# The context scan in a tile of its own, the ada modulation moved from the loop to the LayerNorm stage, late gelus in their own buffers

## The chip, the cores and the metric

One core of a Trainium2 chip runs the kernel. The metric is device time in microseconds of one execution, taken as the median of several; the kernel before took 882.67 us (three runs, 881.9 to 884.6). A core has a matrix engine (TensorE, PE in the profile), three engines for element-wise work (VectorE or DVE, ScalarE or ACT, GpSimd or POOL) and a queue that issues the DMAs here (SyncE, SP). Each engine takes its instructions in the order of the program and they wait for each other through semaphores.

## The reference

One layer of a diffusion backbone over 512 latent tokens with 256 context tokens, width 1024. What is computed, cut to its core:

```python
sh1, sc1, gt1, sh2, sc2, gt2 = split(silu(c) @ w_ada + b_ada)      # the ada modulation, 6 x 1024
hl = rmsnorm(x, g_pre_mix) * (1 + sc1) + sh1                       # hc: the same for the context, with c_ctx
glu, xr, gt, (ga, gb) = split(hl @ w_in)
# RG-LRU, both directions d, context first, then the latent tokens from its last state:
r, i = sigmoid(xr_d @ w_r + b_r), sigmoid(xr_d @ w_i + b_i)        # xr after a conv of width 4
a = exp(-8 * r * softplus(-lam)); u = sqrt(1 - a * a) * i * xr
h[t] = a[t] * h[t - 1] + u[t];  rec = h_forward + h_backward
y_a = silu(layernorm(conv31(v * sigmoid(g)))) @ w_proj_conv
y_b = (rec * gelu(gt)) @ w_proj_lru
x = x + gt1 * rmsnorm((sigmoid(ga) * y_a + sigmoid(gb) * y_b) @ w_out, g_post_mix)
h = rmsnorm(x, g_pre_ffn) * (1 + sc2) + sh2
x = x + gt2 * rmsnorm((silu(g) * v) @ w_down, g_post_ffn)          # v, g: 3x3 depthwise conv of h @ w_up
```

## The kernel before, in words

Channels lie on the 128 partitions, tokens along the free dimension; a width of 1024 is 8 blocks. Every matmul of the network is done in three (mm3, lines 133 to 136): each float32 operand is split into a rounded high part and the remainder, and high x high, low x high and high x low are summed in PSUM. Weights are split on the way in: SP loads a raw tile (line 105, a ring of 3), ACT writes whi (line 122) and POOL, for some DVE, writes wlo = raw - whi (line 123, rings of 4). The function queue lists all weights in one fixed order, and W(key, look, ahead) splits up to `look` weights ahead of the one that is wanted and loads `ahead` further. cvt_to and dma_to do it for one index. The order of every engine's instructions is that of the program text.

PSUM has two tags for matmuls: mm2 (two tiles of two banks) and mm1 (two of one bank); cv tiles (two) belong to the convolution and to small things. A tile that is asked for waits until the last reader of the one whose place it takes. The same holds for SBUF pools that are opened where others were closed: the side "right" is a stack, and with reuse_waits="tile" a new tile waits for the old tiles whose addresses it overlaps.

The stages, in time of the profile: start, norms and first blocks (0 to 100 us); the loop over the eight channel blocks b of the recurrence (lines 665 to 742, 76 to 293 us); gelus, ga, gb, yb (lines 744 to 802, to 402 us); LayerNorm stage (lines 814 to 876, to 442 us); ya and its output projection (to 545 us); the ConvFFN (to the end).

An iteration b of the loop does on PE: block xr for b (24 matmuls of 512 columns and 24 of 262 for the context), gate_mm for block b - 1 (direction 0, r), block v, gate_mm (0, i) and (1, r), block g, gate_mm (1, i). Each gate_mm takes an mm2 tile, as xr does, so xr of b + 1 takes the place of gate (1, r), whose last reader is DVE's L612 of that direction. ACT does the gates' tanh in place (L597), the decay a (L604), another tanh (L605) and a square (L607); the square roots of block b - 2 (L623, with a table load before and after). DVE does conv31 in portions (fill, L520), the width-4 convolution (L568 to L575), L612 and L616, the products L629 and the scans of block b - 2: L634 over the context in place in u, L635 over the latent tokens into rec, starting from the context's last column, L636 backwards over both. POOL does wlo, xl (L140), the other L629 and the sum of both directions (L637).

Inside iterations 2 to 5 a share of the ada modulation (the 1024 values of sh2) is done: two tiles `wa` of weights are loaded (L715, tag wa of pool pl, 8 KB), PE multiplies them into the free quarter of the last gate's PSUM tile (ada_pe, L303), and DVE sums into ggb (L731, L733); iteration 6 transposes the sum into adl (ada_cols, L320, L321). The share sc2 is done in the LayerNorm stage instead: tiles in the place of later w_out weights (ada_dma, L806), two groups of four (ada4), into the PSUM tile acc4.

After the loop gt_act applies gelu to the eight gate branches: 0 to 4 in their SBUF copies, 5 to 7 from PSUM into sa (L653). Then gt_post multiplies with rec (L658) and splits the product on ACT (rgh) and DVE or POOL (rgl, L140) for the yb blocks. offload does a few taps of the convolution on ACT and POOL (L544, L546). ga_act writes tanh of ga into sa (L774).

Of the kernel before, what the change touches and what calls it, by code (L numbers as in the profile page):

```python
# [37 lines left out]
def backbone_kernel(es: ExitStack, tc: tile.TileContext, x, ctxt, par, wadq, wada, win, wgate, wpc, wpl, wout,  # L38
# [459 lines left out]
    pl = es_r.enter_context(tc.tile_pool(name="pl", bufs=2, side="right", reuse_waits="tile"))  # L498

# [131 lines left out]
    def scans(b):  # L631
        (a0, _), (a1, _) = lru[b, 0], lru[b, 1]
        u0, u1 = lru[b, 0, 1], lru[b, 1, 1]
        V.tensor_tensor_scan(u0[:, T:TA], a0[:, T:TA], u0[:, T:TA], 0.0, ALU.mult, ALU.add)  # L634
        V.tensor_tensor_scan(rec[:, b, :], a0[:, 0:T], u0[:, 0:T], u0[:, TA - 1:TA], ALU.mult, ALU.add)  # L635
# [15 lines left out]
    def gt_act(b):  # L651
        t = gts[b] if b < 5 else sa[:, b, :]
        S.activation(out=t, in_=gts[b], func=AF.Gelu_apprx_tanh)  # L653
        gts[b] = t
# [10 lines left out]
    for b in range(1, NB + 1):  # L665
# [46 lines left out]
        if 2 <= b <= 5:  # L712
            for k in (2 * b - 4, 2 * b - 3):
                was[k] = pl.tile([128, D], F32, tag="wa", name="wa")
                nc.sync.dma_start(out=was[k], in_=wada[1, :, k, :])  # L715
# [10 lines left out]
        ps = gate_mm(b - 1, 1, 1)  # L726
        if 2 <= b <= 5:
            o = ps[:, TA:1024]
            ada_pe((2 * b - 4, 2 * b - 3), (was[2 * b - 4], was[2 * b - 3]), o, True, True)
            if b == 2:  # L730
                V.tensor_copy(ggb[:, 0:256], o)  # L731
            else:
                V.tensor_add(ggb[:, 0:256], ggb[:, 0:256], o)  # L733
        if b == 6:
            ada_cols(3, ggb[:, 0:256])(ps[:, T:1024])
# [12 lines left out]
    for b in range(5):  # L748
        gt_act(b)
# [29 lines left out]
    gt_act(5)  # L779
    gt_act(6)  # L780
    gt_act(7)
    gt_post(range(NB))
    offload(4)
    yb = pd.tile([128, NB, T], F32, tag="d", name="yb")
    for b in (0, 1):
        ga_act(b)
    for b in range(-1, NB):
# [16 lines left out]
    def ada_dma(k):  # L804
        was[k] = pw1.tile([128, D], F32, tag=f"wo{k // 2 % 2}{'hl'[k % 2]}", name="wa")
        nc.sync.dma_start(out=was[k], in_=wada[2, :, k, :])  # L806

    def ada4(ks):
        ada_pe(ks, [was[k] for k in ks], acc4[:, 0:256], ks[0] == 0, ks[-1] == NB - 1)
        for k in ks:  # L810
            if k < 4:
                ada_dma(k + 4)

    for b in (2, 3):
# [4 lines left out]
    for k in range(4):  # L819
        ada_dma(k)  # L820
# [19 lines left out]
    ada4(range(4))  # L840
# [9 lines left out]
    ga_mm(5, range(6, NB))  # L850
    ga_mm(6, look=1)
# [8 lines left out]
    for b in range(NB):  # L860
# [6 lines left out]
        if b == 3:  # L867
            ga_mm(7)
# [4 lines left out]
    ada4(range(4, NB))  # L873
# [24 lines left out]
    for b in range(NB):  # L898
# [3 lines left out]
        if b in (0, 3):  # L902
            rest()
# [342 lines left out]
```

## Time and profile before

| | us |
|---|---|
| median of three runs | 882.67 |
| profiled execution, its own time | 883.99 |
| its span, first to last instruction | 882.2 |
| PE busy in the span | 854.5 |
| DVE, ACT, POOL busy | 663.0, 430.7, 412.7 |
| mean granted TensorE clock | 0.993 |

The profile is a record of one execution: for each instruction its engine, line, tiles, start and length, the idle time of the engine before it and what ended that. From it come a list of groups of instructions, a list of waits, the chain of work that ended last, timelines of one engine, and sums over stretches. A matmul's length in the record is longer than the spacing of two, since they overlap; read the starts. The granted clock is 1.00 at 2.4 GHz and 0.50 at 1.2 GHz.

### The profile page before, as it was taken

The numbers are of one execution on the slowest core, as the hardware profiler recorded it, in microseconds if no ns is written. First come the engines' busy times: TensorE is split into PE (matmuls) and PEld (weight loads), VectorE is DVE, ScalarE is ACT, GpSimd is POOL, SyncE is SP. The second block draws the span as 40 slices with busy tenths as digits, with TensorE's granted clock in tenths as the row PEclk, the third lists the DMA queues.
The fourth block names the chain that finished last, engine by engine and source line by source line (L and its number), as shares of the span: only waits on it lengthen the run. The fifth ranks groups of instructions, "written<-read, shape, count | busy, mean of one in ns | idle before, by whom it ended". The sixth has DMA issues, their size and how long they took to land.

```text
span 882.2 us, 11379 instructions
## 1 busy us (share of the span) xinstructions
PE 854.5 (97%) x4312; PEld 691.3 (78%) x4312; DVE 663.0 (75%) x932; ACT 430.7 (49%) x614; POOL 412.7 (47%) x227
## 2 busy tenths in 40 slices
PE   7999999999899889999999999999999999999997
PEld 6777877877787668887778889888888888888785
DVE  4355899999997999994465345899998998998204
ACT  5273766866677742223753345634534344345222
POOL 1234545655456574545343212536645556457820
PEclk9999999999999999999999999999999999999999
DMA  9952133222222222224454411223432333333402
GB/s 351 371 216 84 61 120 132 108 99 68 72 84 72 95 96 96 94 86 156 167 167 144 166 48 48 96 85 119 143 119 85 124 112 112 113 113 124 163 0 96
DMA packets 31398, 106.01 MB, mean 120 GB/s; under 512 B 3440, under 2 KB 3568, under 8 KB 31344
## 3 DMA queue, kind: packets, MB, share of 16 engines
q1 hardware_dynamic: 31344, 105.29, 33.9%
q8 instruction: 34, 0.56, 0.3%
q14 instruction: 20, 0.16, 0.1%
HBM read 103.17 MB, written 2.10 MB: 119 GB/s over the span
## 4 chain that ended last, share of the span: by engine, by line
PE 75%; DVE 11%; ACT 8%; issue 3%; POOL 1%; DMA 0%; DVEq 0%; SPq 0%; ACTq 0%
PE up_ps L135 8%; PE up_ps L134 8%; PE up_ps L136 8%; DVE cv L520 3%; DVE rec L635 3%; PE ya_ps L134 2%; PE y_ps L135 2%; PE yb_ps L136 2%; PE yb_ps L135 2%; PE yb_ps L134 2%; PE ya_ps L136 2%; PE ya_ps L135 2%; PE y_ps L134 2%; PE y_ps L136 2%; PE gb_ps L136 2%
## 5 line engine op out<-in xcount | busy, mean ns | idle before, releaser
L123 POOL TENSOR_TENSOR wlo<-raw,whi 128x1024 fp32r<-128x1024 f32 x117 | 290.4, 2495 | 221.6 <-ACT whi L122 221.4
L1040 DVE SCALAR_TENSOR_TENSOR cv<-zall,P,cv 128x512 f32<-128x512 f32 x240 | 161.8, 743 | 0.2
L520 DVE SCALAR_TENSOR_TENSOR cv<-glu,P,cv 128x512 f32<-128x512 f32 x228 | 153.8, 745 | 0.0
L122 ACT ACTIVATE whi<-raw 128x1024 fp32r<-128x1024 f32 x121 | 125.0, 1052 | 21.0 <-issue 8.0
L134 PE MATMUL up_ps<-Ahi,whi 128*128 128x512 f32 (+1 forms) x352 | 131.8, 374 | 0.0
L135 PE MATMUL up_ps<-Alo,whi 128*128 128x512 f32 (+1 forms) x352 | 131.7, 374 | 0.0
L136 PE MATMUL up_ps<-Ahi,wlo 128*128 128x512 f32 (+1 forms) x352 | 131.6, 374 | 0.0
L135 PEld LDWEIGHTS up_ps<-Alo,whi 128*128 128x128 f32 x352 | 66.0, 188 | 13.3
L136 PEld LDWEIGHTS up_ps<-Ahi,wlo 128*128 128x128 f32 x352 | 66.0, 188 | 13.2
L134 PEld LDWEIGHTS up_ps<-Ahi,whi 128*128 128x128 f32 x352 | 66.0, 188 | 13.1
L1026 POOL TENSOR_TENSOR acl<-fo,ach 128x512 fp32r<-128x512 f32 x20 | 26.0, 1300 | 85.5 <-ACT ach L1023 85.5
L1040 DVE SCALAR_TENSOR_TENSOR cv<-zall,P,cc 128x512 f32<-128x512 f32 x40 | 43.1, 1105 | 21.2 <-ACT cc L1014 21.2
L1012 ACT ACTIVATE zall<-up_ps 128x512 f32<-128x512 f32 x40 | 23.7, 592 | 63.5 <-PE up_ps L136 63.5
L597 ACT ACTIVATE gate_ps<-gate_ps,P 128x768 f32<-128x768 f32 x32 | 27.9, 873 | 47.5 <-DVE ggb L733 19.1
L1023 ACT ACTIVATE ach<-fo 128x512 fp32r<-128x512 f32 x20 | 12.7, 633 | 66.8 <-DVE fo L1022 66.8
L140 POOL TENSOR_TENSOR xl<-xc,xh 128x768 fp32r<-128x768 f32 x8 | 14.9, 1858 | 45.9 <-ACT xh L139 45.9
L364 ACT ACTIVATE tg<-gb_ps 128x512 f32<-128x512 f32 x8 | 4.8, 596 | 60.2 <-PE gb_ps L136 60.2
L134 PE MATMUL xr_ps<-Ahi,whi 128*128 128x512 f32 x56 | 23.3, 416 | 5.6 <-DVE e L612 5.6
L136 PE MATMUL gb_ps<-Ahi,wlo 128*128 128x512 f32 x64 | 26.0, 407 | 2.5 <-POOL wlo L123 2.5
L1014 ACT ACTIVATE cc<-up_ps,P 128x512 f32<-128x512 f32 x40 | 27.3, 682 | 1.8 <-DVE cv L1040 1.8
L1040 DVE SCALAR_TENSOR_TENSOR fo<-zall,P,cv 128x512 f32<-128x512 f32 x40 | 27.8, 734 | 0.0
L134 PE MATMUL ga_ps<-Ahi,whi 128*128 128x512 f32 x64 | 26.0, 406 | 1.6 <-ACT sa L653 1.6
(391 smaller groups left out, 2127.0 us busy)
## 6 DMA issues: line engine op xcount, KB each, us to landing
raw<-in_win_dram SPq DMA_DIRECT2D x48, 512.0 KB, 3.3
raw<-in_wup_dram SPq DMA_DIRECT2D x40, 512.0 KB, 3.3
wa<-in_wada_dram SPq DMA_DIRECT2D x24, 512.0 KB, 5.7
raw<-in_wdn_dram SPq DMA_DIRECT2D x22, 512.0 KB, 3.3
wa<-in_wadq_dram SPq DMA_DIRECT2D x16, 512.0 KB, 8.1
raw<-in_wpl_dram SPq DMA_DIRECT2D x8, 512.0 KB, 3.2
raw<-in_wpc_dram SPq DMA_DIRECT2D x8, 512.0 KB, 3.8
raw<-in_wout_dram SPq DMA_DIRECT2D x8, 512.0 KB, 3.3
```

Source lines behind the costliest of these rows:

```text
L122: S.activation(out=flat(hl[0]), in_=flat(t), func=AF.Copy)
L123: eng.tensor_sub(flat(hl[1]), flat(t), flat(hl[0]))
L134: PE.matmul(o, lh, rh, start=first, stop=False)
L135: PE.matmul(o, lh, rl, start=False, stop=False)
L136: PE.matmul(o, ll, rh, start=False, stop=last)
L520: V.scalar_tensor_tensor(out=cv[b] if k else glu[:, b, 0:T], in0=glu[:, b, k:k + T], scalar=col("dw31", 31 * b + k, 1), in1=cv[b], op0=ALU ...
L597: S.activation(out=lru[b, d, q], in_=lru[b, d, q], func=AF.Tanh, scale=0.5, bias=hb[:, i:i + 1])
L635: V.tensor_tensor_scan(rec[:, b, :], a0[:, 0:T], u0[:, 0:T], u0[:, TA - 1:TA], ALU.mult, ALU.add)
L1012: S.activation(out=z[:, 1:1 + GH, 1:1 + GW], in_=ps.rearrange("p (r c) -> p r c", c=GW), func=AF.Copy)
L1014: S.activation(out=c, in_=ps.rearrange("p (r c) -> p r c", c=GW), func=AF.Copy, scale=col("dw9", 9 * (i + FW * (1 - s)) + 4, 1))
L1026: G.tensor_sub(acl[:, i, :], fo[i, 0], ach[:, i, :])
L1040: V.scalar_tensor_tensor(out=o, in0=zz[i, s][:, k // 3:k // 3 + GH, k % 3:k % 3 + GW], scalar=col("dw9", 9 * (i + FW * (1 - s)) + k, 1), i ...
```

## The change

Four things. scans writes the context scan into a tile hc of its own (1 KB, two buffers in pl) and takes the start value from there. The ada work of sh2 leaves the loop, with its loads, additions and transposes; instead the LayerNorm stage loads all 16 weight tiles in four groups (ada_dma, ada4): sc2 in groups 0 and 1, sh2 in groups 2 and 3, the first loads being issued before ga 2, and each of the two sums is copied out of acc4 and transposed in the ya stage, where rest now runs at b = 0, 1 and 2 instead of 0 and 3. The gelus 5 to 7 go to a new pool pge (three buffers of 2 KB) and all eight follow the last scans in the text, ahead of the new pools. And the split of weight gb 1 is put before gt_post, that of yb 0 after it, both ahead of ga_act and offload.

```diff
--- before.py
+++ after.py
@@ -496,6 +496,7 @@
     block(ps1[:, 0:T], W(("xr", 1), 1, 2), Ahi, Alo)
     es_q.close()
     pl = es_r.enter_context(tc.tile_pool(name="pl", bufs=2, side="right", reuse_waits="tile"))
+    pge = es_r.enter_context(tc.tile_pool(name="pge", bufs=3, side="right", reuse_waits="tile"))
 
 
     lacc = [None]
@@ -631,8 +632,9 @@
     def scans(b):
         (a0, _), (a1, _) = lru[b, 0], lru[b, 1]
         u0, u1 = lru[b, 0, 1], lru[b, 1, 1]
-        V.tensor_tensor_scan(u0[:, T:TA], a0[:, T:TA], u0[:, T:TA], 0.0, ALU.mult, ALU.add)
-        V.tensor_tensor_scan(rec[:, b, :], a0[:, 0:T], u0[:, 0:T], u0[:, TA - 1:TA], ALU.mult, ALU.add)
+        hc = pl.tile([128, TC], F32, tag="hc", name="hc")
+        V.tensor_tensor_scan(hc, a0[:, T:TA], u0[:, T:TA], 0.0, ALU.mult, ALU.add)
+        V.tensor_tensor_scan(rec[:, b, :], a0[:, 0:T], u0[:, 0:T], hc[:, TC - 1:TC], ALU.mult, ALU.add)
         V.tensor_tensor_scan(u1[:, TA - 1::-1], a1[:, TA - 1::-1], u1[:, TA - 1::-1], 0.0, ALU.mult, ALU.add)
         (V if b == 7 else G).tensor_add(rec[:, b, :], rec[:, b, :], u1[:, 0:T])
 
@@ -649,7 +651,7 @@
         gts[b] = t
 
     def gt_act(b):
-        t = gts[b] if b < 5 else sa[:, b, :]
+        t = gts[b] if b < 5 else pge.tile([128, T], F32, tag="ge", bufs=3, name="ge")
         S.activation(out=t, in_=gts[b], func=AF.Gelu_apprx_tanh)
         gts[b] = t
 
@@ -709,10 +711,6 @@
         i_dve(b - 1, 0)
         if b + 1 < NB:
             glu_mul(tg, psv, b + 1)
-        if 2 <= b <= 5:
-            for k in (2 * b - 4, 2 * b - 3):
-                was[k] = pl.tile([128, D], F32, tag="wa", name="wa")
-                nc.sync.dma_start(out=was[k], in_=wada[1, :, k, :])
         if b + 2 < NB:
             psg = mm1("g_ps")
             block(psg, W(("g", b + 2)), Ahi, Alo)
@@ -723,16 +721,7 @@
         fill(3)
         r_dve(b - 1, 1)
         fill(3)
-        ps = gate_mm(b - 1, 1, 1)
-        if 2 <= b <= 5:
-            o = ps[:, TA:1024]
-            ada_pe((2 * b - 4, 2 * b - 3), (was[2 * b - 4], was[2 * b - 3]), o, True, True)
-            if b == 2:
-                V.tensor_copy(ggb[:, 0:256], o)
-            else:
-                V.tensor_add(ggb[:, 0:256], ggb[:, 0:256], o)
-        if b == 6:
-            ada_cols(3, ggb[:, 0:256])(ps[:, T:1024])
+        gate_mm(b - 1, 1, 1)
         gate_tanh(b - 1, 1, 1)
         if not last:
             xcs[b] = xc_new
@@ -745,7 +734,7 @@
     gt_block(7)
     scans_mul(7)
     scans(7)
-    for b in range(5):
+    for b in range(NB):
         gt_act(b)
     es_r.close()
 
@@ -776,14 +765,13 @@
     turn[0] = 1
     ga_mm(0)
     ga_mm(1, look=1)
-    gt_act(5)
-    gt_act(6)
-    gt_act(7)
+    cvt_to(index["gb", 1])
     gt_post(range(NB))
-    offload(4)
+    cvt_to(index["yb", 0])
     yb = pd.tile([128, NB, T], F32, tag="d", name="yb")
     for b in (0, 1):
         ga_act(b)
+    offload(4)
     for b in range(-1, NB):
         if b + 1 < NB:
             psg = mm_any("gb_ps")
@@ -801,23 +789,27 @@
         fill(7)
         offload(2)
     gs2 = const.tile([128, 8], F32, name="gs2")
-    def ada_dma(k):
-        was[k] = pw1.tile([128, D], F32, tag=f"wo{k // 2 % 2}{'hl'[k % 2]}", name="wa")
-        nc.sync.dma_start(out=was[k], in_=wada[2, :, k, :])
-
-    def ada4(ks):
-        ada_pe(ks, [was[k] for k in ks], acc4[:, 0:256], ks[0] == 0, ks[-1] == NB - 1)
-        for k in ks:
-            if k < 4:
-                ada_dma(k + 4)
-
+
+    wk = [(2, k) for k in range(NB)] + [(1, k) for k in range(NB)]
+
+    def ada_dma(n):
+        was[n] = pw1.tile([128, D], F32, tag=f"wo{n // 2 % 2}{'hl'[n % 2]}", name="wa")
+        nc.sync.dma_start(out=was[n], in_=wada[wk[n][0], :, wk[n][1], :])
+
+    def ada4(g):
+        ns = range(4 * g, 4 * g + 4)
+        ada_pe([wk[n][1] for n in ns], [was[n] for n in ns], acc4[:, 0:256], g % 2 == 0, g % 2 == 1)
+        if g < 3:
+            for n in ns:
+                ada_dma(n + 4)
+
+    for n in range(4):
+        ada_dma(n)
     for b in (2, 3):
         ga_mm(b, range(NB if b < 3 else 4))
         fill(7)
     ga_act(2)
     fill(1000)
-    for k in range(4):
-        ada_dma(k)
     mean, acc4 = cv_tile("mean"), cv_tile("ada_cp")
     PE.matmul(mean, ones, lacc[0], start=True, stop=True)
     ga_mm(3, range(4, NB))
@@ -837,7 +829,7 @@
     V.tensor_add(sq[:, 1, :], sq[:, 1, :], sq[:, 7, :])
     V.tensor_add(sq[:, 0, :], sq[:, 0, :], sq[:, 1, :])
     cvt_to(index["ga", 6])
-    ada4(range(4))
+    ada4(0)
     big = cv_tile("var")
     for t in range(4):
         PE.matmul(big[:, t:t + 1], sq[:, 0, 128 * t:128 * t + 128], ones[:, 0:1], start=True, stop=True)
@@ -848,6 +840,8 @@
     spread(big, rv, 4)
     rl = big
     ga_mm(5, range(6, NB))
+    ada4(1)
+    rest4 = ada_cols(4, acc4[:, 0:256], acc4)
     ga_mm(6, look=1)
     ga_act(4)
     ga_act(5)
@@ -865,13 +859,14 @@
         if b > 1:
             ln_lo(b - 2)
         if b == 3:
+            ada4(2)
             ga_mm(7)
         if b == 5:
             cvt_to(index["ya", 0])
     ln_lo(6)
     ln_lo(7)
-    ada4(range(4, NB))
-    rest = ada_cols(4, acc4[:, 0:256], acc4)
+    ada4(3)
+    rest = [rest4, ada_cols(3, acc4[:, 0:256], acc4)]
     for b in (6, 7):
         ga_act(b)
 
@@ -899,11 +894,11 @@
         ps = mm_any("ya_ps")
         block(ps, W(("ya", b), 0), slh, sll)
         cvt_to(index["ya", min(b + 2, 7)] if b < 7 else index["wo", 5])
-        if b in (0, 3):
-            rest()
+        if b < 3:
+            rest[b]()
         ya_post(b, ps)
         if b == 1:
-            rest = ada_rows(2, "g_post_mix", ggb)
+            rest += [ada_rows(2, "g_post_mix", ggb)]
             V.scalar_tensor_tensor(out=gs2, in0=adl[:, 32:40], scalar=1.0, in1=col("g_pre_ffn"), op0=ALU.add, op1=ALU.mult)
     es_s.close()
```

## Rows read from the trace of the kernel before

**Rows 1.** The page, part 1: TensorE's busy time, share of the span, instructions.

```profile
PE 854.5 (97%) x4312; PEld 691.3 (78%) x4312; DVE 663.0 (75%) x932; ACT 430.7 (49%) x614; POOL 412.7 (47%) x227
```

**Rows 2.** Waits of PE: who for whom, total us, times, longest us.

```profile
PE xr_ps L134 <- DVE e L612: 5.6, 5, 1.9
```

**Rows 3.** Timeline of PE, loop: start us, length us, what, [idle before <-releaser].

```profile
100.42 0.39 PE L134 MATMUL xr_ps<-Ahi,whi 128*128 128x512 f32 x1
...
124.44 1.07 PE L303 MATMUL gate_ps<-wa,sT 128*32 128x256 f32 x16
...
125.88 0.50 PE L134 MATMUL xr_ps<-Ahi,whi 128*128 128x512 f32 x1 [0.37 <-DVE e L612]
...
153.04 0.50 PE L134 MATMUL xr_ps<-Ahi,whi 128*128 128x512 f32 x1 [1.12 <-DVE e L612]
```

**Rows 4.** Timeline of ACT, iterations 2 and 4 of the loop.

```profile
110.20 0.88 ACT L597 ACTIVATE gate_ps<-gate_ps,P 128x768 f32<-128x768 f32 x1
...
155.33 0.88 ACT L597 ACTIVATE gate_ps<-gate_ps,P 128x768 f32<-128x768 f32 x1 [6.37 <-DVE ggb L733]
...
164.54 0.86 ACT L597 ACTIVATE gate_ps<-gate_ps,P 128x768 f32<-128x768 f32 x1
```

**Rows 5.** Timeline of DVE, iteration 2 of the loop.

```profile
105.89 1.49 DVE L629 TENSOR_TENSOR u<-u,e 128x768 f32<-128x768 f32 x1 [0.76 <-ACT e L623]
...
115.34 3.24 DVE L635 TENSOR_TENSOR_SCAN rec<-a,u 128x512 f32<-128x512 f32 x1
...
118.50 1.73 DVE L636 TENSOR_TENSOR_SCAN u<-a,u 128x768 f32<-128x768 f32 x1
...
124.89 0.94 DVE L612 SCALAR_TENSOR_TENSOR e<-e,gate_ps 128x768 f32<-128x768 f32 x1
```

**Rows 6.** Timeline of POOL, iteration 2 of the loop.

```profile
114.74 2.76 POOL L123 TENSOR_TENSOR wlo<-raw,whi 128x1024 fp32r<-128x1024 f32 x1 [3.20 <-ACT whi L122]
```

**Rows 7.** Timeline of PE after the loop, ga 1 and gb 1.

```profile
302.47 0.50 PE L134 MATMUL ga_ps<-Ahi,whi 128*128 128x512 f32 x1 [1.58 <-ACT sa L653]
...
313.78 0.40 PE L134 MATMUL gb_ps<-Ahi,whi 128*128 128x512 f32 x1
...
314.01 0.40 PE L135 MATMUL gb_ps<-Alo,whi 128*128 128x512 f32 x1
...
316.95 0.79 PE L136 MATMUL gb_ps<-Ahi,wlo 128*128 128x512 f32 x1 [2.55 <-POOL wlo L123]
```

**Rows 8.** Windows: length; PE, PEld, DVE, ACT, POOL busy; granted clock; DMA.

```profile
234.50:238.10 3.60, 3.59 (x9) 2.81 (x10) 2.58 (x5) 1.56 (x3) 0.00 (x0) 0.53 0.01 2
...
299.40:302.90 3.50, 1.92 (x9) 1.25 (x8) 3.47 (x3) 1.08 (x3) 0.71 (x1) 1.00 0.47 149
...
316.60:320.00 3.40, 3.04 (x7) 2.47 (x8) 3.40 (x5) 0.00 (x0) 3.40 (x3) 0.51 0.44 152
```

**Rows 9.** Timeline of ACT after the loop.

```profile
301.82 1.58 ACT L653 ACTIVATE sa<-gt_ps 128x512 f32<-128x512 f32 x3 [4.19 <-DVE u L636]
...
312.35 2.00 ACT L122 ACTIVATE whi<-raw 128x1024 fp32r<-128x1024 f32 x2
```

**Rows 10.** Timeline of DVE after the loop.

```profile
297.76 3.97 DVE L636 TENSOR_TENSOR_SCAN u<-a,u 128x768 f32<-128x768 f32 x1
...
312.91 4.54 DVE L140 TENSOR_TENSOR rgl<-sa,rgh 128x512 fp32r<-128x512 f32 x2
```

**Rows 11.** The chain that ended last, LayerNorm stage: start, us, what.

```profile
422.53 1.86 PE ada_cp L303 x32
...
426.88 0.89 PE var L329 x8
```

**Rows 12.** DMAs of line 806, second group of weights: issue to landing.

```profile
DMA to landing us min/median/max: 3.5/4.7/5.9
```

**Rows 13.** Timeline of ACT, LayerNorm stage.

```profile
431.12 0.82 ACT L863 ACTIVATE glu<-glu,P 128x512 f32<-128x512 f32 x1
```

**Rows 14.** All DMAs into tiles wa: issue to landing.

```profile
DMA to landing us min/median/max: 2.6/5.3/12.0
```


## Prediction

> **What bounds the kernel now.** I read the page first: TensorE (PE) is busy 97% of a span of 882.2 us [rows 1], so time can come only from where PE waits, from slow PE clock, or from PE work that goes. The list of waits names what PE waited for; the reader is to see there that the largest item is the first xr matmul of a loop iteration waiting for DVE's L612, 5.6 us in 5 waits [rows 2]. Then I laid PE, ACT, DVE and POOL of the loop side by side. Call X(b) the moment PE starts block xr of iteration b: X(2) = 100.42, X(3) = 125.88, X(4) = 153.04 [rows 3], and three more periods like the last (X(5) to X(7)). So iteration 2 took 25.46 us and iterations 3 to 6 took 27.16 us each.
>
> Iteration 2 shows the chain that closes an iteration: xr and the first gate on PE, ACT's L597 at 110.20 = X+9.78 [rows 4], three more ACT steps, DVE's first L612, scans L634 to L636, fillers, second L612 ending at 124.89 + 0.94 = 125.83, and xr of iteration 3 starts 0.05 later [rows 3, 5]. PE itself had finished its own work at 124.44 and then did 1.07 us of the ada modulation [rows 3], which lay inside its wait. In iteration 4 the same L597 stands at 164.54 = X+11.50, 1.72 later, and that is the 1.70 by which the period is longer. The reason is one step back: the last gate's L597 sat idle 6.37 us for DVE's ggb addition (L733), which reads the same PSUM bank, and came only at 155.33 = X+2.29 [rows 4]. From there ACT was the late one.
>
> After the loop PE stands twice more: 1.58 us before ga_mm(1) for a gelu (L653) and 2.55 us for POOL's wlo of gb 1 [rows 7]. The gelu into sa had itself waited 4.19 us for the last scan L636 [rows 9], because sa lies where the loop's tiles lay. The clock counts too: after the wait before X(7) it was granted 0.53 in 234.5 to 238.1, after the wait for wlo 0.51 in 316.6 to 320.0; the wait of 1.58 us left it at 1.00 [rows 8].
>
> **Part 1, ggb out of the loop.** The additions go, so L597 of the last gate starts when PE is done, some 1.3 us ahead of X (PE ready at 124.44, X(3) at 125.88) instead of 2.29 behind it. That is 3.6 us earlier where 1.7 are needed, so ACT is no longer late; next is the chain of iteration 2, 25.46. The 1.07 us of PE work itself brings nothing here: PE then only waits longer, 1.5 us per iteration. What could be late next is DVE with POOL: L629 took 1.49 in iteration 2 beside a wlo of POOL, and POOL's own L629, the other direction's, followed [rows 5]. With ACT earlier, that POOL instruction (as long as a wlo, 2.4 to 2.8 [rows 6]) comes ahead of DVE's; DVE then waits up to about 2 us there instead of 0.55. It has some room (0.76 of it was waiting for the square root), so the period rises by 0 to 0.4. I take 25.65, the middle: 4 x (27.16 - 25.65) = 6.0 us gained, bounds 5.2 and 6.8. The loop's 8 DMAs on SP go too; PE, ACT and DVE show no wait for them.
>
> **Part 2, the clock at X(7).** 3.6 us at 0.53 cost 3.6 x 0.47 = 1.6 us of dense PE work [rows 8]. The wait there was 1.9 [rows 2]; with the change it is 25.65 less PE's own 24.0 (100.42 to 124.44) = 1.65, next to the 1.58 that kept the clock. I take all 1.6, bounds 0 and 1.6. PE sets the pace from there to the end of the loop (the chain of waits is PE's own from 234.5 on), so the gain is passed on.
>
> **Part 3, hc.** The scan L635 took 3.24 us for 512 columns, while L636 did 768 in 1.73 [rows 5]: by that rate it needs 1.2, so 2.0 us are a wait. I read it as POOL's: wlo runs 114.74 to 117.50 [rows 6], and 117.50 + 1.08 is the scan's end. In the last block L636 itself took 3.97 [rows 10] with a wlo beside it. L634 writing its own tile leaves the scan's two SBUF inputs, its wait for L634's result and the order on ACT and POOL as they are. The bounds are 0 and 2.0 us per iteration; I take 0, because the start of that wlo hangs on the same ACT step as the scan. The Trainium skill says the same ("SBUF — State Buffer", "Who interferes with whom"): a DVE instruction with two SBUF inputs contends with a GpSimd instruction that reads SBUF, and the lock is exclusive. It speaks against this part of the change, and the trace agrees: 3.24 beside a POOL instruction, while the 768-column scan without one took 1.73. By the rule this part brings 0; were it wrong, the sum would be that of the first rival.
>
> **Part 4, gelus and weights.** The gelus of gt 5 to 7 follow the first five at once, without L636; ga_mm(1) no longer waits: 1.58. wlo of gb 1 came late because its ACT half ran at 312.35, behind all of gt_post [rows 9]; now it is split ahead, and POOL has it by about 305: 2.55. With these the slow clock of 316.6 to 320.0 goes, 3.4 x 0.49 = 1.6. In sum 5.7. Some is given back. pl loses 8 KB and gains 2, pge takes 6, so the end of that stack is where it was and sa overlaps the new ge buffers: ga_act(0) must wait until gt_post's last subtraction has read them. DVE finished that at 312.91 + 4.54 = 317.45 [rows 10]; the two early wlo's share the port with gt_post (they delay it by about 2.4) and the wlo's and offload additions that delayed it before come later (about as much), so I leave it at 317.5. ACT stands behind it with ga_act, four offload steps and the split of gb 2. PE reaches yb 0 at 302.47 - 1.6 + 3 blocks of 24 matmuls at 0.23 us (5.6 each) = 317.7 [rows 7], needs ga_act(0)'s PSUM tile at 318.3, and then wlo of gb 2, about 1.5 us late by the same count (four offload steps of the size of a gelu, 0.5 or a little more, the split of 1.0 [rows 9], POOL's 2.4 to 2.8). I put both at 1.9 us, bounds 0 (tiles not held) and 3.2. Net 5.7 - 1.9 = 3.8, bounds 2.5 and 5.7.
>
> **Part 5, ada in the LayerNorm stage.** Two more groups of 32 narrow matmuls at 1.86 us [rows 11] on a PE that has no gap there: 3.7, and two transposes and a copy, 0.2; the loop's copy of this work was inside waits, so nothing is set against it. Now the DMAs. Group 2 of weights is issued as group 1's tiles are used, by 422.53 + 1.86 = 424.4, and lands 3.5 to 5.9 us after [rows 11, 12]; the last of four is there by about 430.5. PE reaches ada4(1) at 427.8 + 6 matmuls = 429.2 and its last quarter at 430.6 [rows 11]: no wait to speak of. Groups 3 and 4 have a whole block (5.6) plus 1.4 as cover: 7.0 against 5.9. SP is held by these DMAs, and behind them queue the loads of ya 0 and 1, which ACT wants in the middle of its silus; they may cost ACT 1 to 1.5. The copy R ahead of the LayerNorm loop holds DVE until 431.1 instead of 427.8, but ACT's first silu came only at 431.12 [rows 13], so the chain moves by 1.1 while PE has 3.7 more to do before ya. I take 4.0 lost, bounds 3.9 and 6 (one late landing).
>
> **Sum.** -6.0 - 1.6 - 0 - 3.8 + 4.0 = -7.4. The profiled execution took 883.99 (span 882.2 and 1.8 around it), so 876.6; it stands 1.3 above the median of 882.67, so the forecast for the median is 875.3. After the LayerNorm stage PE is dense to the end, so nothing is lost on the way. The bounds of the terms together give -1.7 to -10.2 if all fall to one side.
>
> **The rivals.**
> (1) hc does free the scan. For: L635 alone among the scans reads a start value that was just written in the same tile. Against: L636's 3.97. Iterations would fall to PE's own 24.0, five of them by 1.6 more: -8, 867.
> (2) DVE becomes the bound in the loop, because POOL meets its two-input steps more often. For: DVE is without a gap in the iterations. Period 26.8 instead of 25.65 leaves 1.4, and the longer PE wait keeps the clock loss: -1.4 - 3.8 + 4.0 = -1.2, 881.5.
> (3) PE's longer waits at each X(b) let the clock fall each time. For: 1.9 did it once. Against: 1.58 did not. Four falls more of 1.6 on the chain and none saved: -6.0 - 3.8 + 4.0 + 6.4 = +0.6, 883.3.
> (4) Slower: ada4(1) to ada4(3) wait for their weights. The place is PE's in-order queue, with ga 6, ga 7 and ya 0 behind. It decides once a landing takes longer than its cover, about 6, 7 and 7 us; the slowest landing of such a tile in the trace is 12.0 [rows 14]. At that, 6 + 5 + 5 = 16 are lost: -7.4 + 16 = +8.6, 891.3. Against: here they took at most 5.9.
>
> **How the numbers follow.** Forecast 0.76, rivals 0.06, 0.08, 0.05, 0.05. Range 870.5 to 881.0: the bounds of the terms (872.5 to 881.0), and a little towards rival 1. About 0.3% (2.6 us) is what a measurement of this kernel can tell from no change; so faster is below 880.0. Faster: 0.74 of the forecast's 0.76 and rival 1, 0.80. Same: the rest of the forecast, rivals 2 and 3, 0.15. Slower: rival 4, 0.05.
>
> **What would show it.** Periods X(3) to X(7) of 25.5 to 25.8, L597 of the last gate without a wait for ggb; L635 still at 3.2 or, if POOL comes first, L634 long in its place; clock 1.00 after X(7); no wait of ga_mm(1) for a gelu and of gb 1 for wlo, but yb 0 or gb 2 waiting 1 to 2 us; 64 more narrow matmuls in the LayerNorm stage with PE idle under 1 us there. Periods above 26.3, PE waiting for wada tiles, or a clock below 1 in the loop would make it wrong.

## The result and the profile of the changed kernel

The changed kernel takes 875.95 us (median of 4 runs, 875.31 to 877.16) beside 882.38 of the kernel before (now four runs); the ratio is 0.9924, with a 95% interval of 0.9903 to 0.9945, that is 4.9 to 8.6 us faster. The forecast was 875.3. The profiled execution took 875.37 us, its span is 873.6.

The table cuts both spans at the same marks on PE: X(2) and X(7), the starts of block xr in iterations 2 and 7; the first matmul of ga 0; that of yb 1; that of the LayerNorm mean; that of ya 0. All in us, from the timelines of PE.

| stretch | before | after | difference | forecast |
|---|---|---|---|---|
| start to X(2) | 100.42 | 98.99 | -1.43 | 0 |
| X(2) to X(7), the loop | 134.09 | 127.69 | -6.40 | -6.0 (Part 1) |
| X(7) to ga 0 | 60.62 | 60.65 | +0.03 | -1.6 (Part 2) |
| ga 0 to yb 1 | 39.58 | 33.93 | -5.65 | -3.8 (Part 4) |
| yb 1 to the mean | 75.60 | 75.56 | -0.04 | 0 |
| mean to ya 0 | 31.86 | 36.37 | +4.51 | +4.0 (Part 5) |
| ya 0 to the end | 440.05 | 440.36 | +0.31 | in Part 5 |
| span | 882.22 | 873.56 | -8.66 | -7.4 |

The first line is not the change's: no instruction ahead of X(2) was edited, and in the experiments below the same stretch took between 98.8 and 101.7 us. It goes with the granted clock near the start, which was 0.50 from 12.8 to 16.1 us in the kernel before and 1.00 there in the change. Of the twelve profiles of this document the five without such a stretch reach X(2) at 98.8 to 99.5 us, the three with one at 99.9 to 100.5, and the four with two at 101.0 to 101.7.

The first line of the page after, against [rows 1]: PE is 97% busy as before, with 3 us less of busy time and as many matmuls.

```profile
PE 851.4 (97%) x4312; PEld 690.1 (79%) x4312; DVE 662.5 (76%) x929; ACT 432.5 (50%) x614; POOL 410.7 (47%) x227
```

**The loop.** First PE's list of waits (who for whom; total us, times, longest), against [rows 2], where L612 is now L613. The wait at xr grew from 5.6 to 6.9 us, although the loop became shorter, because PE no longer does ada work inside it; and nothing of ga or gb 1 stands in the list any more, against 1.58 and 2.55 in [rows 7].

```profile
PE xr_ps L134 <- DVE e L613: 6.9, 5, 1.4
...
PE gt_ps L134 <- DVE e L613: 1.5, 1, 1.5
```

Then the timelines of the loop (start, length, what, idle before and releaser): PE at X(2), X(3) and X(4), against [rows 3].

```profile
98.99 0.39 PE L134 MATMUL xr_ps<-Ahi,whi 128*128 128x512 f32 x1
...
124.45 0.50 PE L134 MATMUL xr_ps<-Ahi,whi 128*128 128x512 f32 x1 [1.38 <-DVE e L613]
...
149.99 0.50 PE L134 MATMUL xr_ps<-Ahi,whi 128*128 128x512 f32 x1 [1.37 <-DVE e L613]
```

ACT in iteration 3, against [rows 4] (L597 is now L598): the step of the first gate and that of the last one.

```profile
134.31 0.88 ACT L598 ACTIVATE gate_ps<-gate_ps,P 128x768 f32<-128x768 f32 x1
...
148.66 0.88 ACT L598 ACTIVATE gate_ps<-gate_ps,P 128x768 f32<-128x768 f32 x1 [2.61 <-PE gate_ps L136]
```

The last gate's L598 waits for PE alone and starts 149.99 - 148.66 = 1.33 us ahead of X(4); in the kernel before it stood 2.29 behind. The first gate's stands at X(3) + 9.86, where the slow iterations had X + 11.50. The periods are 25.46, 25.54, 25.56, 25.58 and 25.56.

DVE and POOL of the same iteration, against [rows 5, 6]: DVE's L630 (before: L629) and the 512-column scan L637 (before: L635), and POOL's instructions beside them.

```profile
129.79 2.03 DVE L630 TENSOR_TENSOR u<-u,e 128x768 f32<-128x768 f32 x1
...
139.46 3.23 DVE L637 TENSOR_TENSOR_SCAN rec<-a,hc,u 128x512 f32<-128x512 f32 x1
142.61 1.73 DVE L638 TENSOR_TENSOR_SCAN u<-a,u 128x768 f32<-128x768 f32 x1
```

```profile
129.15 1.86 POOL L630 TENSOR_TENSOR u<-u,e 128x768 f32<-128x768 f32 x1
...
138.86 2.75 POOL L123 TENSOR_TENSOR wlo<-raw,whi 128x1024 fp32r<-128x1024 f32 x1 [4.77 <-ACT whi L122]
```

POOL's L630 now comes ahead of DVE's, which takes 2.03 instead of 1.49. The 512-column scan still takes 3.23 us, and it ends 1.08 us after POOL's wlo, as before.

**Behind the loop.** Windows of the changed kernel (length; PE, PEld, DVE, ACT, POOL busy with counts; granted clock; DMA share; GB/s), against [rows 8]: 3.6 us from X(7); 3.4 us after a wait of 1.50 us in gt block 7; and the place of gb 2.

```profile
226.68:230.28 3.60, 3.60 (x15) 2.92 (x16) 3.60 (x6) 3.57 (x5) 3.23 (x2) 1.00 0.03 13
...
280.20:283.60 3.40, 3.40 (x9) 2.63 (x10) 3.40 (x5) 3.37 (x5) 0.20 (x1) 0.50 0.48 154
...
314.00:317.60 3.60, 3.49 (x16) 2.53 (x15) 3.60 (x6) 1.40 (x2) 3.60 (x2) 1.00 0.17 31
```

The clock held at X(7), and fell to its lower level, 1.2 GHz, in gt block 7 instead. PE at the start of gt block 7, before and after, behind the same wait:

```profile
289.43 0.50 PE L134 MATMUL gt_ps<-Ahi,whi 128*128 128x512 f32 x1 [1.52 <-DVE e L612]
...
280.07 0.70 PE L134 MATMUL gt_ps<-Ahi,whi 128*128 128x512 f32 x1 [1.50 <-DVE e L613]
```

The timeline of ACT, against [rows 9]:

```profile
287.25 1.55 ACT L655 ACTIVATE ge<-gt_ps 128x512 f32<-128x512 f32 x3
288.69 2.01 ACT L122 ACTIVATE whi<-raw 128x1024 fp32r<-128x1024 f32 x2
...
308.05 1.09 ACT L763 ACTIVATE sa<-ga_ps 128x512 f32<-128x512 f32 x2 [5.43 <-DVE rgl L140]
```

The gelus 5 to 7 run at 287.25 without a wait, the halves of gb 0 and gb 1 follow, and ga_act stands 5.43 us for gt_post's last subtraction, which frees the buffers that sa overlaps.

**The LayerNorm stage.** The pieces of the chain that are ada groups (start, length, what), against [rows 11], and below them ACT's first silu, against [rows 13].

```profile
409.04 1.86 PE ada_cp L303 x32
...
415.69 1.43 PE ada_cp L303 x24
417.15 0.64 PE ada_cp L303 x8
...
423.58 1.86 PE ada_cp L303 x32
...
431.24 2.03 PE ada_cp L303 x32
```

```profile
418.91 0.82 ACT L857 ACTIVATE glu<-glu,P 128x512 f32<-128x512 f32 x1 [1.28 <-DVE glu L856]
```

Twelve of the tiles wa now land in this stage; the view of DMAs of this stretch, against [rows 12, 14]:

```profile
L797 SPq DMA_DIRECT2D wa<-in_wada_dram x12: 328/372/1352, 409.7 to 425.6; - x12
...
DMA to landing us min/median/max: 3.6/5.3/7.0
```

### The profile page after: what moved, and what is told of

The parts are those of the page before. It is cut to its first block, busy times and chain, and to the rows that moved or that the text cites. A ratio compares the mean times of both kernels' runs of the same rounds, so it can differ in the third digit from the quotient of the medians.

```text
span 873.6 us, 11376 instructions
## 1 busy us (share of the span) xinstructions
PE 851.4 (97%) x4312; PEld 690.1 (79%) x4312; DVE 662.5 (76%) x929; ACT 432.5 (50%) x614; POOL 410.7 (47%) x227
## 4 chain that ended last, share of the span: by engine, by line
PE 79%; DVE 11%; ACT 5%; issue 3%; DMA 0%; POOL 0%; DVEq 0%; SPq 0%; ACTq 0%; POOLq 0%
PE up_ps L135 9%; PE up_ps L136 9%; PE up_ps L134 9%; PE xr_ps L134 3%; DVE rec L637 3%; PE xr_ps L135 3%; PE xr_ps L136 2%; DVE cv L521 2%; PE ya_ps L134 2%; PE y_ps L135 2%; PE ya_ps L136 2%; PE y_ps L134 2%; PE ya_ps L135 2%; PE y_ps L136 2%; PE yb_ps L134 1%
## 5 line engine op out<-in xcount | busy, mean ns | idle before, releaser
L598 ACT ACTIVATE gate_ps<-gate_ps,P 128x768 f32<-128x768 f32 x32 | 28.0, 875 | 34.2 <-PE gate_ps L136 33.7
L140 POOL TENSOR_TENSOR xl<-xc,xh 128x768 fp32r<-128x768 f32 x8 | 14.9, 1859 | 27.5 <-ACT xh L139 27.5
L134 PE MATMUL gt_ps<-Ahi,whi 128*128 128x512 f32 x64 | 26.0, 407 | 1.5 <-DVE e L613 1.5
L136 PE MATMUL gt_ps<-Ahi,wlo 128*128 128x512 f32 x64 | 25.9, 404 | 0.3 <-POOL wlo L123 0.3
```

Of the source, the lines that this page charges most:

```text
L134: PE.matmul(o, lh, rh, start=first, stop=False)
L136: PE.matmul(o, ll, rh, start=False, stop=last)
L598: S.activation(out=lru[b, d, q], in_=lru[b, d, q], func=AF.Tanh, scale=0.5, bias=hb[:, i:i + 1])
```

## The experiments

Ten kernels ran. Above each result stands what was expected of it before it ran: a theory and a rival, with the time that each would give. Each ratio is to runs of the kernel before on the same chip. Several chips were used, and on them the medians of the kernel before were 882.38 to 884.07, so a difference of medians between two rows can hold up to 1.7 us of the chip; the stretches of the second table are the safer comparison.

| kernel | median us | ratio | 95% interval |
|---|---|---|---|
| the change | 875.95 | 0.9924 | 0.9903 to 0.9945 |
| scan_in_place | 876.72 | 0.9923 | 0.9903 to 0.9943 |
| pe_work_back | 877.43 | 0.9934 | 0.9917 to 0.9951 |
| pe_work_and_read_back | 885.77 | 1.0028 | 1.0016 to 1.0039 |
| early_split | 869.52 | 0.9843 | 0.9824 to 0.9863 |
| gelu_in_sa | 876.50 | 0.9916 | 0.9890 to 0.9943 |
| splits_late | 884.02 | 1.0009 | 0.9994 to 1.0024 |
| ggb_only | 881.52 | 0.9972 | 0.9958 to 0.9985 |
| ln_two_groups | 872.04 | 0.9875 | 0.9840 to 0.9910 |
| sqrt_first | 867.48 | 0.9815 | 0.9788 to 0.9841 |
| early_last_too | 865.67 | 0.9787 | 0.9769 to 0.9804 |

The loop, and the two stretches behind it, cut at the marks of the first table (us):

| kernel | X(2) to X(7) | X(7) to ga 0 | ga 0 to yb 1 | yb 1 to mean | mean to ya 0 |
|---|---|---|---|---|---|
| before | 134.09 | 60.62 | 39.58 | 75.60 | 31.86 |
| the change | 127.69 | 60.65 | 33.93 | 75.56 | 36.37 |
| scan_in_place | 127.71 | 60.61 | 33.95 | 75.54 | 37.54 |
| pe_work_back | 127.75 | 59.07 | 35.46 | 75.60 | 37.12 |
| pe_work_and_read_back | 134.10 | 60.43 | 35.46 | 75.53 | 37.34 |
| early_split | 120.23 | 60.63 | 33.91 | 75.56 | 36.83 |
| gelu_in_sa | 127.73 | 59.08 | 33.57 | 77.73 | 36.63 |
| splits_late | 127.73 | 60.62 | 41.35 | 75.60 | 36.41 |
| ggb_only | 127.68 | 59.07 | 39.80 | 75.59 | 37.01 |
| ln_two_groups | 127.69 | 59.08 | 35.45 | 75.57 | 32.45 |
| sqrt_first | 120.24 | 56.26 | 36.33 | 75.53 | 36.52 |
| early_last_too | 120.26 | 56.29 | 34.41 | 75.53 | 36.72 |

**What made the loop long: PE's ada work, or the read of its bank?** The first kernel puts matmuls of the same size back into the last gate's bank, and nothing reads them; the second also reads the bank.

```diff
 pe_work_back:
-        gate_mm(b - 1, 1, 1)
+        ps = gate_mm(b - 1, 1, 1)
+        if 2 <= b <= 5:
+            o = ps[:, TA:1024]
+            for k in (0, 1):
+                for j in range(4):
+                    PE.matmul(o[32 * j:32 * j + 32, :], sT[:, k, :], P[:, 0:256], start=k == 0, stop=k == 1)
 pe_work_and_read_back, also:
+            V.tensor_copy(ggb[:, 0:256], o)
```

> The changed kernel with the loop's PE work of the ada modulation put back as dead work: after the last gate of iterations 2 to 5 eight narrow matmuls (two groups of four) on parameters already in SBUF go to the same free quarter of the gate's PSUM tile, and nobody reads them (the real work of the LayerNorm stage stays). Theory (the PE work lay inside PE's wait for L613): the periods of the loop stay at 25.5 to 25.6, PE's wait at each X shrinks from 1.5 to about 0.4 us, the time stays at 876 within 1 us. Rival (the gain of the loop came from the PE work): each of four periods rises by about 1.1 us, the time to about 880.4.

> The kernel with the dead PE work and, on top, one DVE copy of that quarter of the PSUM tile at the place where the addition into ggb stood (0.41 us each). Theory (the gate's tanh waits for DVE's read of its bank, and ACT is then late for the next iteration): the tanh of the last gate sits idle 6.4 us for the copy, the four periods from X(3) to X(7) go back to 27.16, +6.4 us, and the clock may fall before X(7), +0 to 1.6: 882 to 884. Rival (what counts is DVE's 0.41 us of work): 4 x 0.41 = +1.6 us, 877.6.

With the work alone the periods stayed at 25.56 to 25.58, and PE's wait for L613 fell to 2.9 us in 5: the work lay inside the wait, as the prediction had it. (The time is 0.4 above the 877 that was allowed; in its profile the stretch to X(2) is 1.5 us longer than in the change and the one from the mean to ya 0 0.75.) With the read the periods were 27.16 again, and the kernel took 8.3 us more (885.77 - 877.43): 6.35 of it in the loop, and 1.4 behind X(7), where the clock fell again. That is above the 882 to 884 expected, which were reckoned from 875.95. ACT and DVE at the end of iteration 3 of that kernel:

```profile
155.94 0.88 ACT L598 ACTIVATE gate_ps<-gate_ps,P 128x768 f32<-128x768 f32 x1 [6.37 <-DVE ggb L730]
```

```profile
153.51 2.06 DVE L521 SCALAR_TENSOR_TENSOR cv<-glu,P,cv 128x512 f32<-128x512 f32 x3
155.48 0.42 DVE L730 COPY ggb<-gate_ps 128x256 f32<-128x256 f32 x1
```

The copy itself takes 0.42 us. It costs 6.4 us of idle ACT because in DVE's queue it stands behind other work, and ACT's tanh on the same bank waits until it is done, though the two use different columns. (Both regions belong to one tile as well as to one bank; no run tells the two reasons apart.) The Trainium skill ("PSUM — Partial Sum Buffer", "PSUM bank collisions raise a hardware error") says that two engines on one bank, in the same partitions, at once collide also at different addresses, and that the compiler's scheduler therefore puts such accesses in order; the trace agrees, with 6.37 us of it here.

**Is the long scan the in-place write, or POOL?** The first kernel undoes hc; the second leaves the change as it is and moves one weight split, so that POOL's wlo runs before the scan and not beside it.

```diff
 scan_in_place:
-        hc = pl.tile([128, TC], F32, tag="hc", name="hc")
-        V.tensor_tensor_scan(hc, a0[:, T:TA], u0[:, T:TA], 0.0, ALU.mult, ALU.add)
-        V.tensor_tensor_scan(rec[:, b, :], a0[:, 0:T], u0[:, 0:T], hc[:, TC - 1:TC], ALU.mult, ALU.add)
+        V.tensor_tensor_scan(u0[:, T:TA], a0[:, T:TA], u0[:, T:TA], 0.0, ALU.mult, ALU.add)
+        V.tensor_tensor_scan(rec[:, b, :], a0[:, 0:T], u0[:, 0:T], u0[:, TA - 1:TA], ALU.mult, ALU.add)
 early_split:
         if not last:
+            cvt_to(index[("v", b + 1) if b + 1 < NB else ("gt", 1)] + 2)
             xw = xr_act(b, ps)
```

> The changed kernel with one part undone: the context scan writes in place in u again, and the latent scan takes its start value from there. Theory (the latent scan waits for POOL, not for its start value): the scan stays at 3.2 us in the blocks of the loop, the periods of the loop at 25.5 to 25.6, and the time at 876 within 1 us. Rival (hc brought something of the gain): the scan's record or the periods change and the time rises by 1 us or more.

> The changed kernel with one split moved: the weight of the next iteration's xr, whose split POOL did while DVE came to the scans, is split before ACT's L563 of the iteration, where ACT waited 1.7 us for PE; POOL is then free when the scans come. Theory (the latent scan waits for POOL's use of the shared port): the scan falls from 3.2 to 1.2 us, the chain of an iteration from 25.5 to 23.5, below PE's own 24.0, so five periods fall by about 1.5 and PE no longer waits for L613 there: 7 to 8 us less, 868 to 869. Rival (the scan is slow by itself, because of its start value or of writing to another tile): it stays at 3.2 and the time at 876 within 1 us.

Undoing hc changed nothing: 0.9923 against 0.9924, periods 25.46 to 25.57, and the scan of iteration 3:

```profile
139.24 3.23 DVE L636 TENSOR_TENSOR_SCAN rec<-a,u 128x512 f32<-128x512 f32 x1
```

With the split moved, the wlo came earlier and the scan took 1.28 us. DVE and POOL of early_split in iteration 3:

```profile
136.83 0.95 DVE L613 SCALAR_TENSOR_TENSOR e<-e,gate_ps 128x768 f32<-128x768 f32 x1
137.70 0.68 DVE L636 TENSOR_TENSOR_SCAN hc<-a,u 128x256 f32<-128x256 f32 x1
138.42 1.28 DVE L637 TENSOR_TENSOR_SCAN rec<-a,hc,u 128x512 f32<-128x512 f32 x1
```

```profile
129.18 2.42 POOL L630 TENSOR_TENSOR u<-u,e 128x768 f32<-128x768 f32 x1
131.64 4.78 POOL L123 TENSOR_TENSOR wlo<-raw,whi 128x1024 fp32r<-128x1024 f32 x2
```

POOL is through with its two wlo at 131.64 + 4.78 = 136.42, ahead of the scan. The periods are 24.01 to 24.07, which is PE's own work, PE has no wait for L613 left at any X(b), and the loop takes 120.23 instead of 127.69 us: 7.5 us less, where the first rival gave 8 for a freed scan. The kernel is 6.4 us faster than the change by the medians (869.52 against 875.95; by the ratios 0.8%, 7.1 us), a little less than the 7 to 8 expected, and the edit is one line.

**Which of the edits behind the loop brings the gain?** Three kernels: the gelus back in sa, with the early splits; the splits late, with the gelus' own buffers; and ggb_only, the kernel before with the ada work of sh2 (ggb) moved to the LayerNorm stage as in the change, and nothing else.

```diff
 gelu_in_sa:
-        t = gts[b] if b < 5 else pge.tile([128, T], F32, tag="ge", bufs=3, name="ge")
+        t = gts[b] if b < 5 else sa[:, b, :]
...
     ga_mm(1, look=1)
     cvt_to(index["gb", 1])
+    for b in (5, 6, 7):
+        gt_act(b)
     gt_post(range(NB))
 splits_late:
     ga_mm(1, look=1)
-    cvt_to(index["gb", 1])
     gt_post(range(NB))
-    cvt_to(index["yb", 0])
+    offload(4)
...
     for b in (0, 1):
         ga_act(b)
-    offload(4)
```

> The changed kernel with the gelus of gt 5 to 7 back in sa and back behind ga_mm(1), and without the three buffers of their own; the early splits of gb 1 and yb 0 stay. Theory (the prediction's Part 4): sa lies where the loop's tiles lay, so the gelus wait for the last backward scan again and PE stands about 1.6 us before ga_mm(1); part of it had been given back by the wait for gt_post behind it, so 1.2 to 1.6 us slower than the changed kernel (875.95), 877.2 to 877.6, up to 879 if the clock falls once more. Rival: the stretch from X(7) to yb 1 is set by DVE and POOL (gt_post, then the wlo of gb 2) whatever PE does; then the wait of ga 1 only takes the place of the later ones and the time is within 0.5 us of 875.95.

> The changed kernel with the splits of gb 1 and yb 0 no longer ahead: the offloading stands before ga_act as in the kernel before; the gelus keep their own buffers. Theory (the prediction's Part 4): ACT's half of the split of gb 1 comes behind all of gt_post, PE waits about 2.5 us for the wlo of gb 1 and then runs some 3.5 us at half clock (1.6 us of work): 3 to 4 us slower than the changed kernel (875.95), 879 to 880. Rival: the stretch is set by the chain of gt_post and the later wlo of gb 2, so that the wait only moves from gb 2 to gb 1: within 1 us, 875.5 to 877.

> The kernel before with one part of the change alone: ggb moved from the loop to the LayerNorm stage. The scan writes in place, the gelus 5 to 7 go into sa, and gb 1 and yb 0 are split where they were. Loop -6.4, LayerNorm stage +4.5, as in the two profiles; open is the stretch behind the loop, 39.6 us from ga 0 to yb 1 in the kernel before. Theory (from gelu_in_sa): the gelus waited for the last scan because two weight tiles in the loop's stack laid sa over the scan's tile; without those tiles they run at once, whatever buffers they have, and the stretch falls by 1.5 to 4 us with the scan-bound wait of PE before ga 1 gone: in all 3.5 to 7 us faster than before. Rival (the prediction's Part 4): only buffers of their own free the gelus; the waits of PE for the gelu (1.6) and for the wlo of gb 1 (2.6) stay, and the time is 2 to 3.4 us under that of before.

gelu_in_sa took 876.50: the same as the change, not 1.2 us more. The gelus into sa did not wait, though the last scan was not over (ACT, then DVE, of gelu_in_sa):

```profile
288.66 1.55 ACT L654 ACTIVATE sa<-gt_ps 128x512 f32<-128x512 f32 x3
```

```profile
288.88 3.97 DVE L637 TENSOR_TENSOR_SCAN u<-a,u 128x768 f32<-128x768 f32 x1
```

ggb_only shows the same (its gelus run at 288.32, its last scan from 288.53). Neither has the new buffers; what both have, and the kernel before lacks, is a loop without the two weight tiles in its stack. So the wait of [rows 9] went with the ggb move. That sa then no longer overlaps the scan's tile is how I explain it; that the buffers are not needed for it is what the runs show.

But freeing ga 1 saves nothing by itself. In ggb_only PE stands later, at gb 1:

```profile
304.24 0.50 PE L134 MATMUL gb_ps<-Ahi,whi 128*128 128x512 f32 x1 [1.39 <-ACT whi L122]
...
307.70 0.51 PE L136 MATMUL gb_ps<-Ahi,wlo 128*128 128x512 f32 x1 [2.72 <-POOL wlo L123]
```

That is 1.39 + 2.72 = 4.1, as much as the 1.58 + 2.55 of [rows 7], again with slow clock behind it (from 308.6), and ga 0 to yb 1 takes 39.80, as before. ggb_only is 2.5 us faster than the kernel before (0.9972): the gelu went free as the theory said, the time came out in the range of the rival, and for neither one's reason.

splits_late took 884.02, 8.1 us more than the change, where 3 to 4 were expected. PE at gb 1:

```profile
310.16 0.80 PE L134 MATMUL gb_ps<-Ahi,whi 128*128 128x512 f32 x1 [3.61 <-ACT whi L122]
```

and ACT just before that:

```profile
308.08 1.08 ACT L763 ACTIVATE sa<-ga_ps 128x512 f32<-128x512 f32 x2 [3.89 <-DVE rgl L140]
309.05 2.00 ACT L122 ACTIVATE whi<-raw 128x1024 fp32r<-128x1024 f32 x2
```

ga_act waits for gt_post because sa lies over the gelus' new buffers, and the split of gb 1 is queued behind it on ACT. PE then waits 3.6 us for whi, 1.3 more for wlo, and runs 6.5 us at a granted clock of 0.50. In ggb_only, where ga_act waits for nothing, the same split came at 303.13. So in this kernel the new buffers without the early splits cost about 3 us (1.0009 against 0.9972), and the early splits without the buffers, on top of the ggb move, give all of the gain (0.9916 for gelu_in_sa).

gelu_in_sa itself is 1.9 us ahead of the change at yb 1 (59.08 + 33.57 against 60.65 + 33.93). Its clock held in gt block 7; that alone is not the reason, since pe_work_back's held too and brought nothing by yb 1. What gelu_in_sa has besides is a ga_act that waits for nothing (303.05, against 308.05 behind the wait of 5.43). It loses 2.1 again at ga 2. There PE waits for a wlo that stands behind additions of POOL:

```profile
395.14 0.50 PE L136 MATMUL ga_ps<-Ahi,wlo 128*128 128x512 f32 x1 [1.91 <-POOL wlo L123]
```

```profile
390.31 2.47 POOL L532 TENSOR_TENSOR lnsum<-lnsum,glu 128x512 f32<-128x512 f32 x2 [7.86 <-DVE glu L520]
392.73 7.04 POOL L123 TENSOR_TENSOR wlo<-raw,whi 128x1024 fp32r<-128x1024 f32 x3
```

POOL's additions had to wait for DVE's fillers, which began 5 us later than in the change (312.82 against 307.86), since gt_post on DVE met more of POOL's work (its six subtractions took 6.92 + 4.59 us, against 7.00 in the change). What was won early was lost 75 us later.

**What do the two groups cost in the LayerNorm stage?**

```diff
-        if g < 3:
+        if g < 1:
...
-            ada4(2)
...
-    ada4(3)
-    rest = [rest4, ada_cols(3, acc4[:, 0:256], acc4)]
+    V.tensor_copy(adl[:, 24:32], col("b_ada", 24, 8))
+    rest = [rest4, lambda: None]
```

> The changed kernel without the two groups of ada work that came from the loop (the share of the modulation that makes sh2 is left out, sh2 is its bias alone). Theory (the prediction's Part 5): PE has no gap in the LayerNorm stage, so two groups of 1.86 us, their transposes and the small gaps about them come off in full: 3.9 to 4.5 us faster than the changed kernel (875.95), 871.4 to 872.1. Rival: the groups lie partly in a wait that PE would have anyway (ACT's silus and DVE's LayerNorm steps ahead of ya 0), so that only 1 to 2.5 us come off, 873.5 to 875.

This kernel leaves out work that the layer needs, the whole of sh2 but its bias, and serves only to price it. It took 872.04, 3.9 us under the change; from the mean to ya 0 it takes 32.45 instead of 36.37 us, 0.6 over the kernel before. So the groups come off in full, as the theory had it.

**The two square-root and split moves of the last iteration**, on top of early_split:

```diff
 sqrt_first:
             gt_block(3)
+            scans_act(b - 2)
             gt_copy(3)
...
-        if b >= 2:
+        if b >= 2 and not last:
             scans_act(b - 2)
 early_last_too, also:
         gate_mm(b - 1, 1, 1)
+        if last:
+            cvt_to(index["gt", 7] + 2)
         gate_tanh(b - 1, 1, 1)
```

> The kernel early_split (869.52) with one move: in the last iteration the square roots of block 6 run on ACT before the copy of gt block 3, on which ACT stood idle for 3 us, instead of behind it. Theory: in the last block the DVE chain hangs on ACT's square root, so the chain comes up to 3 us earlier, the wait of PE in gt block 7 (1.5 us) and the slow clock after it (1.5 us of work) shrink: 866 to 869. Rival: the stretch is set by DVE's own work to the end of gt_post, so that an earlier square root brings nothing: 869.5 within 0.5.

> The kernel sqrt_first (867.48) with ACT's half of one more weight split in the last iteration put ahead of the last gate's tanh, so that POOL's wlo comes before the scans of block 7 and not beside the 512-column one. Theory (POOL's port lock): that scan takes 1.3 us instead of 3.25, the DVE chain to gt_post is 2 us earlier, and PE's waits at gb 1 and gb 2 (1.4 and 1.1) shrink: 1 to 2.5 us faster, 865 to 866.5. Rival: gt_post's own steps run into POOL's next two wlo either way (10.4 us for eight multiplications), so that the 2 us are lost there: 867.5 within 0.6.

sqrt_first: PE's wait in gt block 7 is gone, and with it the slow clock: X(7) to ga 0 takes 56.26 instead of 60.63 us. Some of it is given back at yb 0 and gb 2 (ga 0 to yb 1 36.33 instead of 33.91). Net 2.0 us, 867.48. early_last_too: the last block's 512-column scan, beside no POOL instruction now, takes 1.28 us instead of 3.25 (the lines are of sqrt_first, then of early_last_too), and 1.9 us come off from ga 0 to yb 1 (34.41), 865.67. Both are as their theories said. This is the fastest version: 0.9787 of the kernel before, and by the medians 10.3 us under the change.

```profile
277.86 3.25 DVE L637 TENSOR_TENSOR_SCAN rec<-a,hc,u 128x512 f32<-128x512 f32 x1
...
278.33 1.28 DVE L637 TENSOR_TENSOR_SCAN rec<-a,hc,u 128x512 f32<-128x512 f32 x1
```

## Why the prediction held, point by point

**Part 1** held in mechanism and size: 6.40 us against 6.0, a period of 25.56 where 25.65 was taken. L598 of the last gate runs 1.3 us ahead of X, and POOL's L630 comes first and makes DVE's take 2.03, as worked out; the wait in that is some 1.1 us, not the 2 allowed for, since two such products that POOL did not hold up took 1.81 in the last block (DVE at 282.79). pe_work_and_read_back shows that the read of the bank, not PE's work, was the cause.

**Part 2** was right about X(7) and lacked a term behind it. The clock at X(7) stayed at 1.00, and the gain was passed on as far as gt block 7, which starts 280.07 - 226.68 = 53.39 us behind X(7), against 289.43 - 234.51 = 54.92 before: 1.5 us. (The prediction's 1.6 is rounded down: 3.6 x 0.47 is 1.7.) But PE's wait of 1.5 us at gt block 7, which the prediction had no term for since it stood in the kernel before too, was followed by full clock there and by 0.50 here: 3.4 x 0.5 = 1.7 us at most, 1.5 by the table. So the stretch X(7) to ga 0 stayed at 60.65. The step "PE sets the pace" holds up to gt block 7 and not behind it. pe_work_back kept its clock there (59.07 to ga 0), then stood 0.4 us at yb 0 for ga_act and 1.0 at gb 2 for POOL's wlo, and reached yb 1 at the same time behind X(7): 59.07 + 35.46 = 94.53, against 60.65 + 33.93 = 94.58 in the change. There the end of gt_post on DVE and the wlo of gb 2 behind it set the time, so the clock lost in gt block 7 cost nothing by yb 1. From the list of waits of pe_work_back:

```profile
PE gb_ps L136 <- POOL wlo L123: 1.0, 1, 1.0
```

Two of the signs that the prediction named came otherwise: yb 0 and gb 2 were to wait 1 to 2 us, which pe_work_back shows and the change does not (0.4), and a clock below 1 in the loop was to speak against it: it came at the loop's end, in gt block 7.

**Part 3** held: hc brings 0 (scan_in_place). The Trainium skill ("SBUF — State Buffer", "Who interferes with whom") says that whoever issues first holds the shared pair of ports for the whole instruction, and the other one waits. The trace agrees: 3.23 us with a wlo started 0.6 us ahead of the scan, 1.28 with none. The first rival's arithmetic was right for a freed scan (the loop fell to PE's own 24.0); its cause was not.

**Part 4** came out at -5.65 against -3.8, within its bounds (-2.5 to -5.7), and two of its steps were off. First, the 1.58 at ga 1 were booked to the gelus' own buffers: they went with the ggb move, and in ggb_only they came back at gb 1. With the gelus free, the gain is that of the early splits; early splits without the ggb move were not run. Second, 1.9 us were to be given back at yb 0 and gb 2. In the profile of the change it was 0.4 (0.27 and 0.1 at gb 2), since PE had already lost 1.5 to the clock and came later by that much; where the clock held, in pe_work_back, ga 0 to yb 1 took 35.46, which is 4.1 less than before and 1.5 given back. So the prediction's two terms hold in pe_work_back (-1.55 and -4.12 against -1.6 and -3.8), and in the change their sum does: -5.62 against -5.4. The wait of ga_act for gt_post's end on DVE [rows 10] came as foreseen, 5.43 us long.

**Part 5**: 4.5 to ya 0, and 0.3 behind it, against 4.0, within the bounds of 3.9 to 6. The groups took 1.86 to 2.07 us each. What the prediction left out is some 0.1 us at the block start behind each group, and two short waits for the last tile of a group: that of group 1 landed at 417.10 and PE took it up at 417.15, 0.2 us late; that of group 3 landed at 432.58 and was taken up at 432.62, 0.1 us late. Across the kernels above with both groups this stretch took 36.4 to 37.5 us. ACT's silus began 1.3 us later relative to the mean, with 1.1 forecast, and the loads of ya held ACT for 0.68 + 0.20 us, with 1 to 1.5 forecast. The fourth rival's late landing did not come: 7.0 us was the longest.

**The sum**: the span fell by 8.7; 7.2 of that lies behind X(2), against 7.4 forecast, and the other 1.4 goes with the slow clock near the start of the profiled execution before. By the medians the gain is 6.4. That the sum is nearer than its terms is partly luck: the loop gave 0.4 more and the LayerNorm stage, with what follows it, cost 0.8 more.

## What to carry to other kernels

When a wait is removed, look for who stands next in the same queue, and at the next meeting point of the engines: the freed ga 1 was worth nothing until the split of gb 1 was put ahead of the steps that wait. A read of 0.4 us can hold another engine for 6 us if it touches the same PSUM bank and is queued behind other work. If a DVE instruction with two SBUF inputs takes twice its time, look at POOL before its dependences, and move POOL's instruction: here one moved line was worth as much as the whole change.

## What the runs showed of the hardware that was not expected

A wait of the same length was followed by either clock. The wait of 1.5 us in gt block 7 is the same in ten profiles (the last gate's final matmul and gt block 7 start 1.8 us apart in all). After it, the granted clock fell to the lower level in four (the change, scan_in_place, early_split, splits_late) and stayed at the upper one in six (before, pe_work_back, pe_work_and_read_back, gelu_in_sa, ggb_only, ln_two_groups). The same window in gelu_in_sa, beside the 0.50 above:

```profile
280.55:283.95 3.40, 3.40 (x15) 2.75 (x16) 3.40 (x5) 3.37 (x5) 0.09 (x1) 1.00 0.49 154
```

What decides between them is left open here.

How much DVE loses beside POOL shows in gt_post. In ggb_only five of its multiplications, none begun while a POOL instruction ran, took 3.09 us (0.68 for one, overlapping a little), so eight would take 4.9. In sqrt_first the eight took 10.44 us, 5.5 more. Two of them, each begun during a wlo of POOL, took 2.90 us, and a third, begun during a subtraction of POOL (L140, 1.61 us), took 1.78; the five others took 0.68 each. Each of the three ended about 0.55 us after the POOL instruction beside it. POOL's two wlo took 5.62 us, against 4.76 for two in splits_late (from 277.03) beside DVE's fillers, which have an input in PSUM; so POOL lost less than 1.

```profile
293.15 3.09 DVE L658 TENSOR_TENSOR ge<-ge,rec 128x512 f32<-128x512 f32 x5
```

```profile
283.41 10.44 DVE L660 TENSOR_TENSOR ge<-ge,rec 128x512 f32<-128x512 f32 x8
```

```profile
283.56 5.62 POOL L123 TENSOR_TENSOR wlo<-raw,whi 128x1024 fp32r<-128x1024 f32 x2 [3.53 <-PE ga_ps L136]
```
